# Memory attention's way out: a written-down DVE order, router logits first, the last tile's norm on ACT and POOL

## The chip, the cores and the metric

One core of a Trainium2 chip runs the whole program in one launch. The metric is device time in microseconds. The program is a two-layer encoder over 512 tokens of width 1024, in fp32.

## The reference, cut to what matters

```python
for i in range(DEPTH):                      # 2 layers
    mix = differential_attention(h, ...) if i % 2 == 0 else dsa_sparse_mla(h, ...)
    h = layer_norm(alpha * h + mix, ln_g[i, 0], ln_b[i, 0])
    h = layer_norm(alpha * h + memory_cross_attention(h, mem_k, mem_v, xa_w_q[i], xa_w_out[i]),
                   ln_g[i, 1], ln_b[i, 1])
    h = layer_norm(alpha * h + hierarchical_moe(h, ...), ln_g[i, 2], ln_b[i, 2])

def memory_cross_attention(x, mem_k, mem_v, w_q, w_out):
    ...                                     # o: softmax over 256 memory rows, 4 heads
    return o @ w_out                        # 512x1024 by 1024x1024

def hierarchical_moe(x, ...):               # 16 experts, two of them for each token
    g_logits = t @ w_group + b_group        # 4 columns
    e_logits = t @ w_expert + b_expert      # 16 columns
    ...
```

The place of the change is the second of the three norms: `o @ w_out`, the sum with `alpha * h`, the norm, and the 20 router logits of the normed row.

## The kernel before, in words

The 512 tokens are four tiles `t` of 128 rows, `hx[t]` (128x1024, fp32, named `xp0x` in layer 0 and `xp1x` in layer 1). A product in full precision is three TensorE products: each weight is split into a high half (ACT copies it to fp32r, L209) and a low half (DVE subtracts, L210); so are the activations. `U.get(name)` splits the next weight unit of a written list and issues the loads of the units behind it on SP's queue; a unit is 1 MB. Raw units share three buffers, those of the expert cells (`cell_r`) have these and two more, and a load waits until the split before it in its buffer is done. The units behind the output weights `w00`, `w01`, `w10`, `w11` are those of the first expert, `mw_0_0` and so on.

Queues of SP and POOL run in the order in which the code is written; DMAs issued there wait in that order too. The order of PE, ACT and DVE around the change is set by a planner that simulates the program, except inside blocks with `manual_schedule(engines=...)`: there the named engines run in written order. `mem_attention` has such a block for PE. At its end PE has already multiplied the first six of eight row blocks of `w_out`'s left half for all four tiles (`begun`).

`out_proj` then finishes the stage. For each half row `hf` and tile `t`: the rest of the product on PE (`proj_part`, L254 to L256, one 128x512 product each); on DVE the sum with `ALPHA * hx` and its row sums (L343, called a close below); `router_part`, which transposes the half row on PE (L673), copies it to SBUF (L678 on ACT for the left half, L676 on DVE for the right) and multiplies it with the router's weights on PE (L681). For the left half DVE keeps the 20 partial logits (L685). After the right half of a tile: `ln_stats` (mean on DVE, L301; Square with row sums on ACT, L305; `rsqrt` in nine small DVE steps, L193 to L202), `router_logits` (three small DVE steps, L689 to L691), `ln_scale` (DVE, 128x1024, L309), `ln_shift` (DVE for 768 columns, L315; POOL for the other 256 in two steps, L318 and L319), `after1` (a store to `h_d` on POOL's queue, L1556, and to `acc_d` on SP's, L1557), and for tiles 0 and 1 `pre`, which splits one unit of the first expert.

PSUM: `mm` tiles (two buffers) take the products of tiles 0 and 1 and all of the right half; tiles 2 and 3 of the left half share one `sc2` pair; `tp` tiles (two buffers) take transposes and logits.

`moe` follows. `router` (L720 to L751) is some 25 small DVE steps over all four tiles; `slot_tokens` makes the first two experts' token lists (L866 to L869), POOL fills the gather tiles (L911) and gathers their rows from `h_d` (L915), so the gather needs the last tile's store. PE turns the rows (L922) and the first expert starts (L937).

## Time and profile before

| | us |
|---|---|
| median of 3 runs (1708.81 to 1712.48) | 1708.97 |
| profiled execution | 1712.64 |
| its span | 1710.9 |
| PE busy | 1560.7 (91%) |
| DVE busy | 1179.8 (69%) |
| ACT busy | 845.5 (49%) |
| POOL busy | 233.7 (14%) |

Times in rows and text are microseconds from the start of the profiled span. PE is TensorE's products, DVE VectorE, ACT ScalarE, POOL GpSimd, SP the queue of SyncE. An engine's idle time counts only where the next stage waits for that engine.

### The profile page before, as it was taken

What the parts mean: (1) busy time and instruction counts of PE and PEld (TensorE: products, weight loads), DVE (VectorE), ACT (ScalarE), POOL (GpSimd) and SP (SyncE); (2) the same over time, 40 slices, a digit from 0 to 9 for tenths busy, and PEclk for the clock granted to TensorE, in tenths of its full rate; (3) what the DMA queues carried; (4) which work ended last, traced back from release to release, by engine and by line L of the source; (5) the groups of instructions that cost most, each with busy time, mean ns of one, the idle gap of its engine ahead of it and who ended that gap; (6) DMA issues with size and microseconds to landing.
All of it is one profiled execution on the core that took longest, in us unless ns stands there. A gap on an engine that the chain in (4) does not pass through costs nothing. (4 is left out here: it accounts for less than half of the span.)

```text
span 1710.9 us, 23216 instructions
## 1 busy us (share of the span) xinstructions
PE 1560.7 (91%) x8572; PEld 1298.0 (76%) x8572; DVE 1179.8 (69%) x2324; ACT 845.5 (49%) x1135; POOL 233.7 (14%) x230
## 2 busy tenths in 40 slices
PE   7999899798995899999997879998999599999995
PEld 6888698697774678888876747798878487888883
DVE  5444545645447898898867699737335899899695
ACT  4343544523331676785754434633332377577582
POOL 1000000111003032221210000002001223132121
PEclk9999899899997899999998989999999699999997
DMA  7130123622325698998975201115141699899894
GB/s 224 50 99 1 48 89 117 215 77 99 127 95 204 236 344 326 306 355 321 314 228 178 95 25 39 49 62 175 50 147 62 241 348 374 296 322 360 287 302 135
DMA packets 118334, 317.58 MB, mean 186 GB/s; under 512 B 23773, under 2 KB 72925, under 8 KB 93632
## 3 DMA queue, kind: packets, MB, share of 16 engines
q1 hardware_dynamic: 100400, 272.00, 45.0%
q0 software_dynamic: 17808, 43.96, 8.3%
q8 instruction: 71, 1.16, 0.3%
q14 instruction: 55, 0.45, 0.1%
HBM read 299.38 MB, written 36.70 MB: 196 GB/s over the span
## 5 line engine op out<-in xcount | busy, mean ns | idle before, releaser
L210 DVE TENSOR_TENSOR cell_l<-cell_r,cell_h 128x2048 fp32r<-128x2048 f32 x192 | 430.8, 2285 | 40.9 <-ACT cell_h L209 40.8
L209 ACT ACTIVATE cell_h<-cell_r 128x2048 fp32r<-128x2048 f32 x192 | 363.5, 1915 | 81.6 <-DMA cell_r<-in_moe_w_up_dram 19.8
L937 PE MATMUL pg<-cell_h,xh 128*128 128x512 f32 x288 | 119.2, 414 | 2.2 <-ACT xh L259 2.2
L965 PE MATMUL py<-cell_h,hsh 128*128 128x512 f32 x288 | 116.1, 403 | 1.4 <-ACTq L1065 1.4
L937 PE MATMUL pg<-cell_l,xh 128*128 128x512 f32 x288 | 116.0, 403 | 0.0
L965 PE MATMUL py<-cell_h,hsl 128*128 128x512 f32 x288 | 113.4, 394 | 0.0
L965 PE MATMUL py<-cell_l,hsh 128*128 128x512 f32 x288 | 113.1, 393 | 0.0
L937 PE MATMUL pu<-cell_h,xh 128*128 128x512 f32 x288 | 112.0, 389 | 0.0
L937 PE MATMUL pu<-cell_l,xh 128*128 128x512 f32 x288 | 112.0, 389 | 0.0
L955 POOL DMA_INDIRECT acc_d<-y,sx x34 | 74.8, 2200 | 156.9 <-ACT y L954 115.1
L915 POOL DMA_INDIRECT xg<-h_d,sx x32 | 42.0, 1312 | 358.1 <-DVE sx L902 328.4
L259 ACT ACTIVATE xh<-xgT 128x1024 fp32r<-128x1024 f32 x36 | 36.8, 1022 | 98.5 <-PE xgT L922 93.3
L937 PE MATMUL pg<-cell_h,xl 128*128 128x512 f32 x288 | 79.1, 397 | 0.0
L937 PE MATMUL pu<-cell_h,xl 128*128 128x512 f32 x288 | 77.0, 389 | 0.0
L937 PEld LDWEIGHTS pg<-cell_h,xh 128*128 128x128 f32 x288 | 56.6, 197 | 14.1 <-ACT xh L259 3.0
L937 PEld LDWEIGHTS pg<-cell_h,xl 128*128 128x128 f32 x288 | 55.7, 193 | 12.4
L937 PEld LDWEIGHTS pg<-cell_l,xh 128*128 128x128 f32 x288 | 56.5, 196 | 11.2
L965 PEld LDWEIGHTS py<-cell_h,hsh 128*128 128x128 f32 x288 | 54.5, 189 | 13.1 <-ACTq L1065 1.8
L965 PEld LDWEIGHTS py<-cell_h,hsl 128*128 128x128 f32 x288 | 54.5, 189 | 12.6 <-DVEq L1065 0.9
L965 PEld LDWEIGHTS py<-cell_l,hsh 128*128 128x128 f32 x288 | 54.6, 190 | 10.6
L937 PEld LDWEIGHTS pu<-cell_h,xh 128*128 128x128 f32 x288 | 54.1, 188 | 11.2
L937 PEld LDWEIGHTS pu<-cell_h,xl 128*128 128x128 f32 x288 | 54.1, 188 | 11.2
(917 smaller groups left out, 4206.1 us busy)
## 6 DMA issues: line engine op xcount, KB each, us to landing
cell_r<-in_moe_w_gate_dram SPq DMA_DIRECT2D x64, 1024.0 KB, 8.0
cell_r<-in_moe_w_up_dram SPq DMA_DIRECT2D x64, 1024.0 KB, 8.1
cell_r<-in_moe_w_down_dram SPq DMA_DIRECT2D x64, 1024.0 KB, 7.2
mhx<-acc_d POOLq DMA_DIRECT2D x8, 512.0 KB, 7.0
x<-in_x_dram SPq DMA_DIRECT2D x4, 512.0 KB, 6.9
g<-in_ln_g_dram POOLq DMA_DIRECT2D x4, 512.0 KB, 4.0
b<-in_ln_b_dram POOLq DMA_DIRECT2D x4, 512.0 KB, 4.0
op0x<-in_x_dram POOLq DMA_DIRECT2D x4, 512.0 KB, 7.6
```

Source lines behind the costliest of these rows:

```text
L209: nc.scalar.activation(hi[:, c], raw[:, c], AF.Copy)
L210: nc.vector.tensor_tensor(lo[:, c], raw[:, c], hi[:, c].bitcast(F32), op=ALU.subtract)
L259: nc.scalar.activation(hi, src, AF.Copy)
L915: nc.gpsimd.indirect_dma_start(out=x, out_offset=None, in_=h_d[:, :], in_offset=bass.IndirectOffsetOnAxis(ap=idx[:, 0:1], axis=0), bounds_ ...
L937: nc.tensor.matmul(o, xT[l][:, a, :], W[r][:, k, :], start=a == l == r == 0, stop=a == 7 and l == 1)
L955: nc.gpsimd.indirect_dma_start(out=acc_d[:, :], out_offset=bass.IndirectOffsetOnAxis(ap=ix[:, 0:1], axis=0), in_=y, in_offset=None, bounds ...
L965: nc.tensor.matmul(o, hs[a][:, ts(2 * q + f)], Dq[b][:, f, c], start=q == f == k == 0, stop=q == f == 1 and k == 2)
```

## The change

`xp_proj` takes the place of `out_proj` for memory attention's way out; `out_proj` stays for the other attentions and loses its options. In `xp_proj` DVE runs in written order: the four left halves with the kept logits and the splits of `w10`, `w11` and the first expert unit between them; then for each tile the right half, the mean, the scale and shift of the tile before (or, at tile 0, the split of the second expert unit), rsqrt and the router's logits. `router_part` copies both halves on ACT and returns its logits tile, which stays in PSUM until `keep` or `router_logits` reads it. The last tile is normed by ACT (`x * rstd + nmr`, where `nmr` is the negative mean times `rstd`) and POOL (times the gain, plus the bias, both 128x1024). The splits of the first expert units, and with them the loads that they issue, are written ahead of the stores.

```diff
--- before.py
+++ after.py
@@ -39,7 +39,6 @@
 DBL = (5, 11)
 HP = 400
 FILL = [["q2"], ["v1", "q3"], ["q4"], ["v2", "q5"], ["m0", "q6"], ["v3", "q7"], ["m1", "m2"], ["m3"]]
-NFIRST = 2
 RING = 6
 RAWS = 5
 DSA0 = ("P0", "P1", "F0 P2", "F1 P3")
@@ -295,15 +294,16 @@
         q.dma_start(b, I["ln_b"][i, j].partition_broadcast(P))
         return g, b
 
-    def ln_stats(hx, sums, name, eps=EPS):
+    def ln_mean(hx, sums, name):
         nmu = small(name + "m", [P, 1])
-        if len(sums) == 2:
-            nc.vector.tensor_scalar(nmu, sums[0], sums[1], -1.0 / D, op0=ALU.add, op1=ALU.mult)
-        else:
-            nc.vector.tensor_scalar(nmu, sums[0], -1.0 / D, None, op0=ALU.mult)
+        nc.vector.tensor_scalar(nmu, sums[0], sums[1], -1.0 / D, op0=ALU.add, op1=ALU.mult)
         ss = small(name + "s", [P, 1])
         nc.scalar.activation(junk, hx, AF.Square, bias=nmu, accum_out=ss)
-        return nmu, rsqrt(ss, 1, name, 1.0 / D, eps)
+        return nmu, ss
+
+    def ln_stats(hx, sums, name):
+        nmu, ss = ln_mean(hx, sums, name)
+        return nmu, rsqrt(ss, 1, name, 1.0 / D, EPS)
 
     def ln_scale(hx, nmu, gb):
         nc.vector.scalar_tensor_tensor(hx, hx, nmu, gb[0], op0=ALU.add, op1=ALU.mult)
@@ -323,36 +323,82 @@
         mm3(o, [(oT[0](k, ts(t)), oT[1](k, ts(t)),
                  W[k // 4][0][:, k % 4, :], W[k // 4][1][:, k % 4, :]) for k in ks], ks[0] == 0, last)
 
-    def out_proj(oT, src, ij, name, after, R=None, pre=None, begun=None):
+    def xp_proj(oT, src, i, after, R, split_first, begun):
+
+        name = f"xp{i}"
+        sums = [[small(f"{name}s{t}{hf}", [P, 1], bufs=2 * NT) for hf in range(2)] for t in range(NT)]
+        gb = load_gb(i, 1)
+        hx = reload(src, f"{name}x")
+        W, o, n0 = begun
+        half = [slice(0, 512), slice(512, D)]
+        lps, stats = {}, {}
+
+        def close(hf, t):
+            proj_part(o[t], oT, W, t, range(n0 if hf == 0 else 0, 8), True)
+            x = hx[t][:, half[hf]]
+            nc.vector.scalar_tensor_tensor(x, x, ALPHA, o[t], op0=ALU.mult, op1=ALU.add, accum_out=sums[t][hf])
+            lps[hf, t] = router_part(R, t, hf, x, f"{name}{t}{hf}")
+
+        def keep(t):
+            nc.vector.tensor_copy(R["lg"][:, t, :], lps.pop((0, t))[:, 0:20])
+
+        def apply(t):
+            ln_scale(hx[t], stats[t][0], gb)
+            ln_shift(hx[t], stats[t][1], gb)
+            after(t, hx[t])
+
+        with tc.manual_schedule(engines={ENG.DVE}):
+            close(0, 0)
+            close(0, 1)
+            W2 = [U.get(f"{name}w10")]
+            keep(0)
+            close(0, 2)
+            keep(1)
+            W2.append(U.get(f"{name}w11"))
+            close(0, 3)
+            keep(2)
+            split_first()
+            keep(3)
+            W, o = W2, {}
+            for t in range(NT):
+                o[t] = mm(f"{name}o1{t}")
+                close(1, t)
+                nmu, ss = ln_mean(hx[t], sums[t], f"{name}ln{t}")
+                if t:
+                    apply(t - 1)
+                else:
+                    split_first()
+                stats[t] = nmu, rsqrt(ss, 1, f"{name}ln{t}", 1.0 / D, EPS)
+                router_logits(R, t, stats[t], lps.pop((1, t)))
+
+            nmu, rstd = stats[t]
+            nmr = small(f"{name}nr", [P, 1])
+            nc.vector.tensor_tensor(nmr, nmu, rstd, op=ALU.mult)
+            nc.scalar.activation(hx[t], hx[t], AF.Identity, bias=nmr, scale=rstd)
+            nc.gpsimd.tensor_tensor(hx[t], hx[t], gb[0], op=ALU.mult)
+            nc.gpsimd.tensor_tensor(hx[t], hx[t], gb[1], op=ALU.add)
+            after(t, hx[t])
+
+    def out_proj(oT, src, ij, name, after):
         sums = [[small(f"{name}s{t}{hf}", [P, 1], bufs=2 * NT) for hf in range(2)] for t in range(NT)]
         gb = load_gb(*ij)
         hx = reload(src, f"{name}x")
         for hf in range(2):
-            early = begun if begun and hf == 0 else None
-            W = early[0] if early else [U.get(f"{name}w{hf}{q}") for q in range(2)]
+            W = [U.get(f"{name}w{hf}{q}") for q in range(2)]
             for t in range(NT):
-                o = early[1][t] if early else mm(f"{name}o{hf}{t}")
-                if begun:
-                    proj_part(o, oT, W, t, range(early[2] if early else 0, 8), True)
-                else:
-                    for q in range(2):
-                        mm3(o[:, q * 256:(q + 1) * 256],
-                            [(oT[0](k, ts(t)), oT[1](k, ts(t)),
-                              W[q][0][:, k, :], W[q][1][:, k, :]) for k in range(8)])
+                o = mm(f"{name}o{hf}{t}")
+                for q in range(2):
+                    mm3(o[:, q * 256:(q + 1) * 256],
+                        [(oT[0](k, ts(t)), oT[1](k, ts(t)),
+                          W[q][0][:, k, :], W[q][1][:, k, :]) for k in range(8)])
                 c = slice(hf * 512, hf * 512 + 512)
                 nc.vector.scalar_tensor_tensor(hx[t][:, c], hx[t][:, c], ALPHA, o, op0=ALU.mult, op1=ALU.add,
                                                accum_out=sums[t][hf])
-                if R:
-                    router_part(R, t, hf, hx[t][:, c], f"{name}{t}{hf}")
                 if hf == 1:
                     stats = ln_stats(hx[t], sums[t], f"{name}ln{t}")
-                    if R:
-                        router_logits(R, t, stats)
                     ln_scale(hx[t], stats[0], gb)
                     ln_shift(hx[t], stats[1], gb)
                     after(t, hx[t])
-                    if pre:
-                        pre(t)
 
     def reload(src, name, tags="abcd", q=nc.gpsimd, t0=0):
         hx = []
@@ -665,29 +711,23 @@
             nc.tensor.matmul(pc[:, 0:40], ones, wg[:, k, :], start=k == 0, stop=k == 7)
         nc.vector.tensor_copy(rc[:, 0:20], pc[:, 0:20])
         nc.vector.tensor_tensor(rc[:, 20:40], pc[:, 20:40], br, op=ALU.add)
-        return dict(w=wg, c=rc, lg=small(f"lgs{i}", [P, NT, 20]), lp=None)
+        return dict(w=wg, c=rc, lg=small(f"lgs{i}", [P, NT, 20]))
 
     def router_part(R, t, hf, x, nm):
         pt = tp(f"hTf{nm}")
         for j in range(4):
             nc.tensor.transpose(pt[:, ts(j)], x[:, ts(j)], ident)
         xT = t2("e", f"hTs{nm}")
-        if hf:
-            nc.vector.tensor_copy(xT, pt)
-        else:
-            nc.scalar.activation(xT, pt, AF.Copy)
+        nc.scalar.activation(xT, pt, AF.Copy)
         lp = tp(f"lg{nm}")
         for j in range(4):
             nc.tensor.matmul(lp[:, 0:20], xT[:, ts(j)], R["w"][:, 4 * hf + j, 0:20], start=j == 0, stop=j == 3)
-        if hf:
-            R["lp"] = lp
-        else:
-            nc.vector.tensor_copy(R["lg"][:, t, :], lp[:, 0:20])
-
-    def router_logits(R, t, stats):
+        return lp
+
+    def router_logits(R, t, stats, lp):
         lg, rc = R["lg"][:, t, :], R["c"]
         nc.vector.scalar_tensor_tensor(lg, rc[:, 0:20], stats[0], lg, op0=ALU.mult, op1=ALU.add)
-        nc.vector.tensor_tensor(lg, lg, R["lp"][:, 0:20], op=ALU.add)
+        nc.vector.tensor_tensor(lg, lg, lp[:, 0:20], op=ALU.add)
         nc.vector.scalar_tensor_tensor(lg, lg, stats[1], rc[:, 20:40], op0=ALU.mult, op1=ALU.add)
 
     def router(i, R):
@@ -1558,11 +1598,11 @@
 
         first = []
 
-        def pre(t):
-            if t < NFIRST:
-                first.append(U.get(f"mw{i}_{ORDER[t][0]}_{ORDER[t][1]}"))
-
-        out_proj(oT, h_d, (i, 1), f"xp{i}", after1, R, pre, begun)
+        def split_first():
+            p, j = ORDER[len(first)]
+            first.append(U.get(f"mw{i}_{p}_{j}"))
+
+        xp_proj(oT, h_d, i, after1, R, split_first, begun)
         gT, W3, D3 = [], [], []
 
         def before():
```

## Rows read from the trace of the kernel before

**Rows 1.** The page, its first part: busy time, share of the span and instructions of each engine.

```profile
PE 1560.7 (91%) x8572; PEld 1298.0 (76%) x8572; DVE 1179.8 (69%) x2324; ACT 845.5 (49%) x1135; POOL 233.7 (14%) x230
```

**Rows 2.** Stretches of the span: from, to (us); length; busy us (and instructions) of PE, of PE's weight loads, of DVE, of ACT and of POOL; granted clock of PE; share of the DMA engines; GB/s. First a piece of memory attention in layer 0, then three stretches of its way out and of the gather in layer 0, then two of layer 1.

```profile
440.00:470.00 30.00, 30.00 (x135) 23.71 (x134) 11.66 (x13) 8.89 (x16) 0.80 (x2) 1.00 0.36 126
...
494.85:528.20 33.35, 33.35 (x177) 28.38 (x177) 16.00 (x49) 6.89 (x10) 1.20 (x1) 1.00 0.10 33
...
528.20:542.20 14.00, 8.15 (x43) 7.00 (x42) 13.69 (x40) 2.37 (x4) 8.00 (x10) 0.61 0.85 320
...
542.20:552.14 9.94, 1.90 (x22) 1.29 (x22) 7.95 (x41) 0.00 (x0) 3.98 (x5) 0.50 0.96 394
...
1318.70:1332.40 13.70, 7.49 (x43) 6.49 (x42) 13.63 (x41) 2.39 (x4) 8.47 (x10) 0.66 0.84 315
...
1332.40:1342.46 10.06, 1.89 (x22) 1.28 (x22) 8.08 (x42) 0.00 (x0) 3.98 (x5) 0.50 0.98 406
```

**Rows 3.** DVE's timeline, layer 0, tail of the stretch: start (us), duration (us), engine, line, operation, out<-in, shapes, count, and in brackets the idle time before it and what ended it. The timelines below have the same columns.

```profile
528.16 0.69 DVE L343 SCALAR_TENSOR_TENSOR xp0x<-xp0x,xp0o 128x512 f32<-128x512 f32 x1 [0.15 <-PE xp0o L256]
...
541.12 0.24 DVE L691 SCALAR_TENSOR_TENSOR lgs<-lgs,rsyxp0ln,rc 128x20 f32<-128x20 f32 x1
...
542.21 0.16 DVE L720 TENSOR_REDUCE rt<-lgs 128x4 f32<-128x16 f32 x1
...
549.92 0.16 DVE L869 TENSOR_SCALAR ix<-pi 128x1 int32<-128x1 f32 x1 [0.28 <-PE pi L867]
```

**Rows 4.** POOL's timeline: the last store and the gather in layer 0, the gather in layer 1.

```profile
544.10 0.61 POOL L1556 DMA_DIRECT2D h_d<-xp0x  x1 [0.30 <-POOL xp0x L319]
...
552.14 1.08 POOL L915 DMA_INDIRECT xg<-h_d,ix  x1 [5.58 <-DVE rt L763]
...
1342.46 1.08 POOL L915 DMA_INDIRECT xg<-h_d,ix  x1 [5.70 <-DVE rt L764]
```

**Rows 5.** DMA. GB/s in 40 slices of the window from 520 to 562 us (1.05 us each); median us from issue to landing of the stores of `xp0x` in that window, and of the stores of `op0x` in the window from 381 to 412; two issues of weight loads on SP's queue.

```profile
GB/s 16 0 0 0 0 8 0 0 0 70 374 211 343 359 300 417 414 449 406 425 425 402 437 429 433 417 406 414 417 410 31 0 78 156 191 113 4 0 0 0
...
h_d<-xp0x POOLq DMA_DIRECT2D x4, 512.0 KB, 9.4
...
h_d<-op0x POOLq DMA_DIRECT2D x4, 512.0 KB, 3.3
...
530.40 1.24 SPq L234 DMA_DIRECT2D cell_r<-in_moe_w_gate_dram  x2
```

**Rows 6.** What single steps take, layer 0: DVE's timeline (the low half of a split, a close, a scale, a shift, the first and the last step of one rsqrt with the copy of logits between them), then one Square on ACT.

```profile
466.61 2.29 DVE L210 TENSOR_TENSOR xp0w10l<-xp0w10r,xp0w10h 128x2048 fp32r<-128x2048 f32 x1 [1.02 <-ACT xp0w10h L209]
...
497.88 0.69 DVE L343 SCALAR_TENSOR_TENSOR xp0x<-xp0x,xp0o 128x512 f32<-128x512 f32 x1 [0.67 <-PE xp0o L256]
...
516.93 0.15 DVE L193 TENSOR_SCALAR rsvxp0ln<-xp0ln1s 128x1 f32<-128x1 f32 x1 [1.08 <-ACT junk L305]
...
518.15 0.18 DVE L685 COPY lgs<-lgxp 128x20 f32<-128x20 f32 x1 [0.24 <-PE lgxp L681]
...
518.94 0.16 DVE L202 SCALAR_TENSOR_TENSOR rsyxp0ln<-rswxp0ln,rsyxp0ln 128x1 f32<-128x1 f32 x1
...
525.55 1.28 DVE L309 SCALAR_TENSOR_TENSOR xp0x<-xp0x,xp0ln0m,g 128x1024 f32<-128x1024 f32 x1
...
526.86 1.02 DVE L315 SCALAR_TENSOR_TENSOR xp0x<-xp0x,rsyxp0ln,b 128x768 f32<-128x768 f32 x1
...
533.40 1.15 ACT L305 ACTIVATE junk<-xp0x,xp0ln3m 128x1024 bf16<-128x1024 f32 x1 [4.07 <-issue]
```

**Rows 7.** PE's timeline, layer 0: transposes of a tile's first half row (L673), the first products of the second half row (L254 to L256), 19 more products left out, the logits of the first tile (L681), the next transposes.

```profile
499.05 0.60 PE L673 MATMUL hTfxp<-ident,xp0x 128*128 128x128 f32 x4
...
499.41 0.47 PE L254 MATMUL xp0o<-xp0w10h,xoTh 128*128 128x512 f32 x1
...
499.72 0.39 PE L255 MATMUL xp0o<-xp0w10l,xoTh 128*128 128x512 f32 x1
...
499.95 0.40 PE L256 MATMUL xp0o<-xp0w10h,xoTl 128*128 128x512 f32 x1
...
504.52 0.96 PE L681 MATMUL lgxp<-wg,hTsxp 128*128 128x20 f32 x8
...
505.33 0.63 PE L673 MATMUL hTfxp<-ident,xp0x 128*128 128x128 f32 x4
```

**Rows 8.** POOL's steps of `ln_shift` (L318, L319) and DVE's steps beside them, layer 0; one DVE step with POOL idle (515.61); one POOL fill of a whole tile.

```profile
515.61 0.24 DVE L689 SCALAR_TENSOR_TENSOR lgs<-rc,xp0ln1m,lgs 128x20 f32<-128x20 f32 x1
...
528.75 0.72 POOL L319 TENSOR_TENSOR xp0x<-xp0x,b 128x256 f32<-128x256 f32 x1
...
528.77 0.74 DVE L689 SCALAR_TENSOR_TENSOR lgs<-rc,xp0ln2m,lgs 128x20 f32<-128x20 f32 x1
...
541.27 1.73 POOL L318 TENSOR_SCALAR xp0x<-xp0x,rsyxp0ln 128x256 f32<-128x256 f32 x1 [0.68 <-DVE rsyxp0ln L202]
...
542.40 0.17 DVE L722 TENSOR_TENSOR rt<-lgs,rt 128x16 f32<-128x16 f32 x1
...
543.08 0.72 POOL L319 TENSOR_TENSOR xp0x<-xp0x,b 128x256 f32<-128x256 f32 x1
...
543.11 0.72 DVE L715 TENSOR_TENSOR rt<-iota,rt 128x16 f32<-128x16 f32 x1
...
554.56 0.96 POOL L911 MEMSET xg<- 128x1024 f32 x1
```

## The prediction

> **What bounds the kernel now.** First the page: PE is busy 91% of the span and DVE 69% [rows 1], so a gain must come from a stretch where PE is not fed. Second the stretch table: the way out of memory attention keeps PE full for 33 us at full clock, then DVE is full for 14 us while PE works at half clock, then PE has 1.9 us of work in 9.9 us [rows 2]; layer 1 shows the same two numbers within 0.3 us. From the last projection product to the gather of the first expert's tokens PE is nearly idle, so that stretch is priced one to one, in both layers.
>
> Third, DVE's timeline there. The last half-row sum (L343) starts at 528.16. `ln_scale` and `ln_shift` of three tiles and three copies of transposed rows are still queued, so the last router logits (L691) come at 541.12, the first router step (L720) at 542.21 and the first token list (L869) at 549.92 to 550.08 [rows 3]. Fourth, POOL's queue: the last `h_d` store issues at 544.10, the gather only at 552.14, 2.06 us after its token list was there [rows 4]. The gather reads `h_d`; the DMA rates show why it waits: some 400 GB/s from 530 until 551.5, then almost nothing [rows 5]. In that burst lie four loads of 1 MB and eight stores of 0.5 MB, 8 MB; at 400 GB/s that is 20 us, and an `h_d` store in it takes 9.4. So before, the last store's landing ends the stretch, with the router's chain 2 us behind it. Both must get shorter.
>
> **The change, part by part,** on layer 0's clock.
>
> *Loads.* The three loads that follow the first weight split, and the one behind the second, are now written ahead of all four `acc_d` stores on SP's queue; before they stood between them [rows 5]. They issue when raw buffers come free, from about 506 to 519 by the order below, and 4 MB at 400 GB/s is 10 us: done by about 525. The last `h_d` store then shares the queues with one `acc_d` store. The same store without load beside it lands in 3.3 us [rows 5]; I take that, and keep the 8.0 us of before (544.10 to 552.1) for a rival. The three `h_d` issues ahead of it stay where they are on POOL's queue.
>
> *First half.* `close(0,0)` and `close(0,1)` run as before, the second from 497.88 to 498.65. The low half of `w10`, which ran at 466.61 in an idle DVE [rows 6], now comes behind it: 2.29 us, to 500.9. PE has its first `w10` product at 499.4 and wants the low half at 499.7 [rows 7]: it waits, and fills part of it with a logits product (0.81 us). I price the rest at 0.8 us. DVE's own chain from there is short: four copies `keep` of 0.2 (L685), two closes of 0.77, `w11` and one expert split of 2.25 each, 6.8 us to 507.7. But each `keep` waits for transposes, an ACT copy and a logits product on PE, whose order a planner sets. Before, it put 22 products between a tile's transposes (499.05) and its logits (504.52), though ACT's copy takes 0.60 [rows 7]: it takes products for cheaper than they are. Now only 54 products exist before `close(1,0)` (six of tile 3, 48 of the two open tiles). I take 46 of them ahead of the fourth logits product: 46 x 0.23 = 10.6, three transposes of 0.36 and three more logits of 0.81: 14.1 us [rows 7]. `close(1,0)` starts at about 515.2. Bounds: 508 (order prompt, DVE's chain) and 519 (all 54 ahead, and PE idle 2 us for `w11`, which is queued behind `keep(1)`).
>
> *Second half.* In written order DVE does for a tile: close 0.73 and mean 0.3, the second split 2.2 (tile 0) or the previous tile's scale and shift 1.31 + 0.94, rsqrt 2.17 with a 0.3 us copy wedged in, so 1.9, and three logit steps 0.55: 5.7 us [rows 6]. ACT's Square (1.15) hides behind scale and shift, the copy of transposed rows is now on ACT, 0.60, idle there. From tile 1 on POOL's `+ b` holds up some small DVE step, 0.5 to 0.7 us (below); I take 0.6. `close(1,3)` starts at 515.2 + 5.7 + 2 x 6.3 = 533.5. PE alone would be there at 532.5: it ended at 528.1, plus 0.8, plus three logits and two transposes that before came later (3.2), plus 0.35 of wait. So DVE sets it. Each logits result keeps one of the two small PSUM buffers until DVE has taken it, and PE's next logits product, with all products queued behind it, waits for that; here DVE is there first, and rival (b) prices it if not. Behind it 6.3 and `nmr` 0.15: 540.0. The router starts there, 2.2 us earlier than before, not 14.
>
> *The last tile's norm.* Its scale and shift (2.25) leave DVE. ACT's pass, bounded by Square on the same size, takes 1.15 [rows 6] and POOL starts at 541.5. The trace has no POOL product of 128x1024. The nearest row is 128x256 in 0.72 us [rows 8]: four times is 2.9; a fill of 128x1024, which reads nothing, takes 0.96. I take 2.6 each, nearer to the same operation. The store issues 0.3 behind, at 547.0, and lands at 550.3.
>
> What do these passes do to DVE? When POOL's 128x256 sum began at 543.08, DVE's L715 began at 543.11 and took 0.72 instead of 0.2; L689 took 0.74 under the sum at 528.75, and 0.24 alone [rows 8]. A DVE step with two SBUF inputs waits until such a sum is over. Under POOL's one-input product (541.27 to 543.00) L722 took its 0.17 [rows 8]: that form doesn't hold it. The new passes have two inputs and are four times as wide, and nearly all router steps have two. So: from 540.0 the router runs 1.8 us, waits to the first pass's end at 544.15, does one step, waits to 546.95. It loses 4.9 us. Undisturbed it needs 7.87 us from L720 to the token list, of which 0.55 was L715's wait: 7.3. The list is there at 540.0 + 7.3 + 4.9 = 552.2, the gather at 552.35. The store (550.3) is hidden behind it. POOL's fills of the gather tiles stand ahead of the gather as before and end by 549.5.
>
> [...]
>
> **The sum.** Before, the gather was at 552.14, now 552.35: +0.2. Layer 1 is the same code; its stretch is 0.2 us shorter up to the gather [rows 2, 4], so +0.3. The splits that leave memory attention (two low halves of 2.29) give nothing there, since DVE ran them while PE was full [rows 2, 6]; without that cover they would give 4.6. Edits that only pass names around cost nothing. The profiled execution took 1712.64, its span 1710.9; the median of the runs is 1708.97. The shift is small against either: 1708.97 + 0.5 = **1709.5 us**. What the runs can tell from no change I take as 0.2%, 3.4 us.
>
> **Rivals.** (a) *POOL's passes hold DVE little*, say because small steps slip in between, as L722 did under L318. Then the store's landing ends the stretch: 540.0 + 7.0 + 3.3 + 0.1 = 550.4, 1.7 us a layer: 1705.6. With PE's order prompt too (`close(1,3)` at 532.5, 1.0 earlier) it is 1703.6. Speaks against: L715 and L689. Prompt order alone gives 1707.5.
> (b) *Logits late on PE.* DVE's order is now fixed, so one late logits product delays `close(1,t)` and all behind it. If `close(1,0)` starts at 519 and the second half waits 1 us more, the router starts at 545 and the gather is at 557: +4.9 a layer, 1719. From 516.7 on it shows as slower. The 22 products of [rows 7] speak for it, the few products that are left against.
> (c) *The store lands last.* Were the store to take 8.0 us as in the burst, the gather is at 555.1: 1715. It decides from 5.2 us on. The loads' place speaks against it.
> (d) *POOL's one-input steps (L318) stop DVE's steps too,* 0.92 us for each of tiles 0 to 2, the 1.73 at 541.27 being 0.8 of wait and 0.9 of work: 2.8 a layer, 1715. L722's row speaks against it. [...]
>
> **Chances.** Forecast with prompt order beside it (within 0.2%): 0.42. Faster, mostly (a): 0.31. Slower: (b) 0.17, (c) 0.06, (d) 0.04, together 0.27. The forecast's own range is 1706 to 1712.5; the range that takes in (a) with prompt order and most of (b) is 1703.5 to 1717.5.
>
> **What the new profile should show.** No expert loads after 525 and a DMA rate that falls between stores. `close(1,0)` near 515 and `close(1,3)` near 533.5, DVE idle under 3 us between them. The first router step near 540 and two router steps of about 2.4 us each, just inside POOL's two passes of 2.3 to 2.9 us. The gather waiting on DVE's token list, not on `h_d`. Wrong if router steps run through POOL's passes (a), if DVE idles on `lgxp` between closes (b), or if the gather waits over 1 us behind the list (c).

## The result and the profile after

The change made the kernel slower: 1723.47 us (median of 5 runs, 1721.37 to 1726.23) against 1712.48 for the kernel before on the same chip, ratio 1.0075 [1.0062, 1.0087]. The forecast was no change, 1709.5. The profiled execution after took 1722.15 us, its span 1720.4.

Executions differ by a few us ahead of the stage, so both traces are read from the stage's own start, the first close (496.52 before, 493.01 after). In us behind it, layer 0:

| | 5th close | 8th close | router's first step | gather | gather, layer 1 |
|---|---|---|---|---|---|
| before | 11.33 | 31.64 | 45.69 | 55.62 | 55.42 |
| forecast | 18.7 | 37.0 | 43.5 | 55.8 | about as layer 0 |
| after | 21.15 | 43.49 | 49.68 | 62.00 | 63.55 |

The gathers come 6.4 and 8.1 us late, 14.5 in all. That is the loss: 0.75% of 1712 is 12.8, and the two medians are 11.0 apart.

The page's first part has hardly moved from [rows 1]; the loss is seen only in its stage.

```profile
PE 1555.2 (90%) x8572; PEld 1293.0 (75%) x8572; DVE 1179.1 (69%) x2315; ACT 852.3 (50%) x1144; POOL 240.3 (14%) x230
```

Stretches of the changed kernel, with the columns of [rows 2]: the stage in layer 0 piece by piece, then a piece of layer 1.

```profile
493.00:514.00 21.00, 20.71 (x114) 17.15 (x113) 9.74 (x14) 4.31 (x5) 0.00 (x0) 1.00 0.45 162
515.00:523.00 8.00, 6.91 (x36) 5.83 (x36) 4.98 (x16) 1.73 (x3) 0.00 (x0) 1.00 0.85 306
523.00:531.00 8.00, 6.90 (x36) 5.86 (x36) 5.45 (x16) 1.73 (x3) 3.02 (x3) 1.00 0.33 132
531.00:543.00 12.00, 5.51 (x24) 4.70 (x24) 10.84 (x38) 3.63 (x7) 6.00 (x6) 0.54 0.29 118
...
1320.40:1323.80 3.40, 3.40 (x10) 2.64 (x9) 3.08 (x12) 0.78 (x3) 2.68 (x3) 0.51 0.00 0
```

Before, PE was full for 33 us and then DVE for 14 [rows 2]. Now PE is full only for the first half. After it neither engine is: from 515 to 531 PE stands 2.19 us and DVE 5.57 of 16, each in turn, and from 531 the last two tiles go through DVE with PE at half clock (0.54). DVE's timeline shows the turns.

```profile
514.07 0.18 DVE L343 COPY lgs<-lgxp 128x20 f32<-128x20 f32 x1 [4.32 <-PE lgxp L724]
514.16 0.68 DVE L339 SCALAR_TENSOR_TENSOR xp0x<-xp0x,xp0o 128x512 f32<-128x512 f32 x1
521.95 0.17 DVE L730 TENSOR_TENSOR lgs<-lgs,lgxp 128x20 f32<-128x20 f32 x1 [2.71 <-PE lgxp L724]
522.31 0.68 DVE L339 SCALAR_TENSOR_TENSOR xp0x<-xp0x,xp0o 128x512 f32<-128x512 f32 x1
530.08 0.17 DVE L730 TENSOR_TENSOR lgs<-lgs,lgxp 128x20 f32<-128x20 f32 x1 [2.16 <-PE lgxp L724]
530.44 0.68 DVE L339 SCALAR_TENSOR_TENSOR xp0x<-xp0x,xp0o 128x512 f32<-128x512 f32 x1
536.50 0.68 DVE L339 SCALAR_TENSOR_TENSOR xp0x<-xp0x,xp0o 128x512 f32<-128x512 f32 x1
542.69 0.17 DVE L760 TENSOR_REDUCE rt<-lgs 128x4 f32<-128x16 f32 x1
544.53 2.03 DVE L749 TENSOR_TENSOR rt<-rt,rt 128x64 f32<-128x64 f32 x1
546.59 2.38 DVE L750 SCALAR_TENSOR_TENSOR rt<-rt,iota 128x64 f32<-128x64 f32 x1
553.99 0.16 DVE L909 TENSOR_SCALAR ix<-pi 128x1 int32<-128x1 f32 x1 [0.28 <-PE pi L907]
```

And PE's timeline, the transposes (L719) and logits (L724) of the second half; the products between them are left out.

```profile
515.00 0.63 PE L719 MATMUL hTfxp<-ident,xp0x 128*128 128x128 f32 x4 [0.96 <-DVE xp0x L339]
...
520.95 0.96 PE L724 MATMUL lgxp<-wg,hTsxp 128*128 128x20 f32 x8
523.15 0.63 PE L719 MATMUL hTfxp<-ident,xp0x 128*128 128x128 f32 x4 [1.24 <-DVE xp0x L339]
...
529.08 0.96 PE L724 MATMUL lgxp<-wg,hTsxp 128*128 128x20 f32 x8
```

This is a ring. PE runs a tile's transposes, 24 products of a later tile and only then the tile's logits (520.95). DVE must take those logits (L730) before it may do the next close (L339), by the written order. PE's next step is that close's transposes, so it stands 1.24 us. The close itself had nothing left to wait for: the 54 products that were open before the fifth close, all 48 of the right half's first two tiles among them, are recorded before 513. One turn is 8.13 us (522.31 to 530.44), where before a close came every 6.77.

POOL's timeline answers to [rows 4], the rates of DMA (520 to 562 us) to [rows 5].

```profile
544.14 2.33 POOL L378 TENSOR_TENSOR xp0x<-xp0x,g 128x1024 f32<-128x1024 f32 x1 [1.95 <-ACT xp0x L377]
546.56 2.34 POOL L379 TENSOR_TENSOR xp0x<-xp0x,b 128x1024 f32<-128x1024 f32 x1
549.19 0.59 POOL L1596 DMA_DIRECT2D h_d<-xp0x  x1 [0.30 <-POOL xp0x L379]
...
555.01 1.09 POOL L955 DMA_INDIRECT xg<-h_d,ix  x1 [3.38 <-DVE oh L906]
```
```profile
GB/s 390 258 55 8 0 0 0 176 347 402 82 0 0 0 0 289 347 363 0 0 0 386 339 273 0 0 0 0 285 351 363 0 0 0 0 78 191 219 55 0
...
h_d<-xp0x POOLq DMA_DIRECT2D x4, 512.0 KB, 4.2
```

The loads are out of the way: the rate falls to nothing between stores, and a store lands in 4.2 us (median) instead of 9.4. So that part of the change did what it says.

### The profile page after: what moved, and what is told of

Its sections match the earlier page's. It is cut to its first block, busy times and chain, and to the rows that moved or that the text cites. A ratio compares the mean times of both kernels' runs of the same rounds, so it can differ in the third digit from the quotient of the medians.

```text
span 1720.4 us, 23234 instructions
## 1 busy us (share of the span) xinstructions
PE 1555.2 (90%) x8572; PEld 1293.0 (75%) x8572; DVE 1179.1 (69%) x2315; ACT 852.3 (50%) x1144; POOL 240.3 (14%) x230
## 5 line engine op out<-in xcount | busy, mean ns | idle before, releaser
L977 PEld LDWEIGHTS pu<-cell_l,xh 128*128 128x128 f32 x288 | 54.1, 188 | 11.2
```

What stands on the lines that cost most here:

```text
L977: nc.tensor.matmul(o, xT[l][:, a, :], W[r][:, k, :], start=a == l == r == 0, stop=a == 7 and l == 1)
```

## The experiments

Theory T: DVE's written order ties DVE to logits that the planner lets PE run late. Rival S: the four splits in that order cost the time. Rival L: the last tile's norm on ACT and Pool costs it, by the DVE steps that Pool holds up (two of them, 2.03 and 2.38 us in the changed kernel) and by the later store. All ratios are to the kernel before, from runs on the same chip; where the intervals of two runs overlap, their times alone don't tell the two apart. The table at the end shows the stage of each run.

**One step moved.** In the changed kernel, tile t's logits go behind the sum of tile t+1:

```diff
-        def close(hf, t):
+        def close(hf, t, late=None):
...
+            if late is not None:
+                router_logits(R, late, stats[late], lps.pop((1, late)))
...
-                close(1, t)
+                close(1, t, t - 1 if t else None)
...
-                router_logits(R, t, stats[t], lps.pop((1, t)))
+            router_logits(R, t, stats[t], lps.pop((1, t)))
```

> The changed kernel, but the router's logits of tile t stand in DVE's order behind the sum of tile t+1 (behind `close(1,t+1)`) instead of in front of it; nothing else is moved. Theory T (DVE's written order waits for logits products that PE runs behind the next tile's 24 products): DVE can take the sum of tile t+1 as soon as its products are there, frees its bank, and PE need not stand idle in front of the next transposes. In the changed kernel the logits took DVE's waits of 2.71, 2.16 us (layer 0) and 2.69, 3.78 us (layer 1); I expect about 3.7 us less from the stage's first close to the router's first step in layer 0 and about 5 us less in layer 1, and a time near 1714 to 1716 us where the changed kernel has 1723. Rival S (the four splits written into DVE's order are what costs): nothing changes, 1722 to 1724 us. [...]

Measured 1719.71 us, 1.0052 [1.0034, 1.0069]. The router starts 48.58 us behind the first close in both layers, 1.1 and 2.7 earlier than in the changed kernel: right in sign, a third and a half of the size that T named. PE no longer stands ahead of the transposes of tile 1, but DVE's wait has not gone, it has moved: the sum of tile 1 is done at 520.41, and then DVE stands 3.69 us for the logits of tile 0 (524.25), with the whole normalization of tile 0 queued behind them. (Part of the 3.69 is PE's clock, 0.63 from 515 to 518.5 in this run.)

```profile
519.72 0.68 DVE L339 SCALAR_TENSOR_TENSOR xp0x<-xp0x,xp0o 128x512 f32<-128x512 f32 x1
...
524.25 0.17 DVE L732 TENSOR_TENSOR lgs<-lgs,lgxp 128x20 f32<-128x20 f32 x1 [3.69 <-PE lgxp L726]
```

S wanted no change before the router, and what L blames all lies behind its first step; the traces show a change ahead of that, but the interval of the ratio overlaps that of the changed kernel, so the time alone decides nothing. Moving this one DVE step did not end the waits, with PE still running the logits behind 24 products.

**The norm back on DVE**, in the changed kernel:

```diff
-            nmu, rstd = stats[t]
...
-            nc.scalar.activation(hx[t], hx[t], AF.Identity, bias=nmr, scale=rstd)
-            nc.gpsimd.tensor_tensor(hx[t], hx[t], gb[0], op=ALU.mult)
-            nc.gpsimd.tensor_tensor(hx[t], hx[t], gb[1], op=ALU.add)
-            after(t, hx[t])
+            apply(t)
```

> The changed kernel, but the last tile's normalization is done on DVE as for the other three tiles (two steps of 1024 columns in front of the router) instead of ACT and Pool. Rival L (the norm on ACT and Pool costs it): the two Pool passes held two small steps of the router for 2.03 and 2.38 us, and the h_d store came to be the last thing that the gather waited for (0.86 us behind the token list). Without them the router starts 2.3 us later (two DVE steps of some 1.15 us) but loses no 4.4 us, and the store is some 3 us earlier: the gather comes about 2 us sooner in each layer, 1718 to 1720 us in all. If L were the whole cause of the loss it would come back to the time of before, 1711 to 1713. Theory T (waits for the logits on PE): no more than those 2 us per layer, because the waits of the two halves all stand ahead of the norm.

Measured 1724.66 us, 1.0079 [1.0060, 1.0098]: nothing came back, where 1718 to 1720 was expected, so L is not the cause of the loss. From the router's first step to the gather it takes 9.66 us instead of 12.32, as expected, but the router's start swings: 53.95 us behind the first close in layer 0, 50.75 in layer 1. In layer 0 PE's granted clock was 0.83 from 519 to 539 us, and that eats the gain; in layer 1, at 1.00 from 1318 to 1335, the gather is 3.2 us sooner than in the changed kernel.

**PE's order written as well,** in both halves; shown is the second.

```diff
-        with tc.manual_schedule(engines={ENG.DVE}):
...
+        with tc.manual_schedule(engines={ENG.DVE, ENG.PE}):
...
+                prod(1, t)
+                sum_(1, t)
+                if t + 1 < NT:
+                    prod(1, t + 1, 8)
+                turn(1, t)
...
+                if t + 1 < NT:
+                    prod(1, t + 1, 8)
+                logit(1, t)
```

> The changed kernel, but PE's order of the stage is written down as well as DVE's: the transposes and logits products of a tile are put between products of the next tile (8 products, transposes, 8 products, logits, 8 products) instead of where the planner puts them, behind all 24. Theory T: DVE's waits in front of the logits of the second half go (2.71 and 2.16 us in layer 0, 2.69 and 3.78 us in layer 1), a part of the 9.8 us of waits in the first half goes too, and PE no longer stands idle in front of the transposes; the router starts some 8 us sooner in each layer than in the changed kernel, the gather comes some 2 us sooner than in the kernel before: about 1706 to 1710 us. Rival S (splits in DVE's order): DVE is as late as before its splits, 1720 to 1724. Rival L (norm on ACT and Pool): 1720 to 1724 as well, since that part is not touched.

Measured 1704.79 us, 0.9979 [0.9962, 0.9996]. Same DVE order with its four splits, same norm, only PE's order differs, and the loss is gone. The router starts at 41.71 in both layers, 8.0 and 9.6 us sooner than in the changed kernel (some 8 was expected), and layer 0's gather comes at 54.02. The time is a little below the 1706 to 1710 that T named.

```profile
493.00:508.00 15.00, 15.00 (x92) 13.13 (x91) 9.82 (x15) 4.31 (x5) 0.00 (x0) 1.00 0.52 176
508.00:515.00 7.00, 7.00 (x38) 5.90 (x37) 5.18 (x16) 1.84 (x3) 0.00 (x0) 1.00 1.01 427
515.00:522.00 7.00, 7.00 (x38) 5.89 (x38) 5.66 (x17) 1.83 (x3) 3.00 (x3) 1.00 0.40 165
```

In these stretches of that run PE has no gap, and DVE's 5.2 to 5.7 us of work a tile lie under it.

**The early splits alone**, in the kernel before:

```diff
         for hf in range(2):
...
+            if pre and hf == 1:
+                for t in range(NFIRST):
+                    pre(t)
...
-                    if pre:
-                        pre(t)
```

> The kernel before with a single part of the change: the two splits of the next stage's first weights are written at the start of the second half instead of behind its first two tiles. The planner keeps the order of DVE. Theory T says that the change's own idea costs nothing by itself and that the loss is the written order: DVE's splits move out of the second half, which was DVE-bound, so the router's first step and the gather come up to 2 us sooner in each layer, bounded by the token list: 1708 to 1712 us against 1712 for the kernel before. Rival S (taking the splits early is what costs, because they hold up the first half's closes or their loads collide with others): slower than the kernel before by several us, towards 1718 or more.

Measured 1705.81 us, 0.9982 [0.9969, 0.9994]. The gain is there but not where it was expected: the router starts at 45.36 instead of 45.69, so DVE's 4.6 us of splits were never in its way. The time is below the 1708 to 1712 that was expected. The gather is at 54.08: 0.3 us of the gain are the router's, and 1.2 are that the gather now follows its token list by 0.86 us instead of 2.06. DMA had nothing left to move when the list was there:

```profile
540.00:544.00 4.00, 0.41 (x10) 0.34 (x10) 3.09 (x14) 0.00 (x0) 2.47 (x3) 0.50 0.66 262
544.00:547.00 3.00, 1.49 (x13) 0.94 (x12) 2.27 (x13) 0.00 (x0) 0.15 (x1) 0.50 0.00 0
```

The gather was issued at 546.85, and DMA had been idle since 544; before, its share was 0.96 up to the gather [rows 2]. S falls: two of the splits are early here without a loss, and in the run before all four stood in the written order without one.

**PE's order and the norm on DVE together:**

> Both of the last experiments' edits at once: PE's order written down, and the last tile normalized on DVE. With PE's order written the router's first step came 41.7 us behind the stage's first close and the gather 54.0 us behind it (55.6 in the kernel before). With the norm on DVE the gather followed the router's first step by 9.6 us instead of 12.3. If the two costs lie one behind the other on the same chain (theory T with the shared port as a second cost), they add: router's first step at some 42.9 us, gather at some 52.5 us, 3.1 us per layer sooner than in the kernel before, so about 0.3 to 0.4% faster than it (1703 to 1706 us where it has 1710). If the norm on ACT and Pool is worth what it takes (rival), this is no faster than the run with PE's order alone: ratio 0.998.

Measured 1702.06 us, 0.9950 [0.9934, 0.9967]; router 42.79, gather 52.46, as expected; the time is a little below the 1703 to 1706 named. The two costs add.

**The written order taken away**, all else as in the changed kernel:

```diff
-        with tc.manual_schedule(engines={ENG.DVE}):
+        if True:
```

> The changed kernel with every part of it but one: DVE's order is not written down, the planner places the steps. Theory T, as the first experiments leave it (the stage is PE-bound; a DVE order that waits for a logits product lets PE stand, and then PE's clock falls): PE is busy without gaps again from the first close to the eighth, as in the kernel before (31.6 us there, 43.5 us in the changed kernel). The norm on ACT and Pool still costs the router 4 us. Router's first step 43 to 46 us behind the first close, gather 54 to 57 us: a ratio of 0.997 to 1.003 to the kernel before. Rival L (the norm on ACT and Pool is what costs): the ratio stays near 1.0075.

Measured 1706.36 us, 0.9977 [0.9965, 0.9989]; 8th close 31.61, router 42.04, gather 54.01. One line of the change makes 1.0075 out of 0.9977, 1% of the time. L falls a second time.

**The norm alone**, in the kernel before, for the last tile:

```diff
-                    ln_scale(hx[t], stats[0], gb)
-                    ln_shift(hx[t], stats[1], gb)
+                    if R and t == NT - 1:
...
+                        nc.scalar.activation(hx[t], hx[t], AF.Identity, bias=nmr, scale=stats[1])
+                        nc.gpsimd.tensor_tensor(hx[t], hx[t], gb[0], op=ALU.mult)
+                        nc.gpsimd.tensor_tensor(hx[t], hx[t], gb[1], op=ALU.add)
```

> The kernel before with one part of the change alone: the last tile is normalized on ACT and Pool. The router starts up to 2.8 us sooner, since DVE loses two steps of 1.75 and 1.01 us, and loses 4.0 us in its two held steps, so the token list comes some 1.2 us later. The h_d store is issued some 3 to 4 us later (two Pool passes of 2.33 us); in the kernel before it took 8.0 us to land, because the DMA queues were full of the next stage's weights, and the gather waited for it. If the store's wait stays 8 us (theory: this part costs), the gather comes 3 to 4 us later in each layer, about 1717 us. If the weights' loads are the bound and drain at the same time in any case (rival), the gather comes some 1 us later, 1712 us and a ratio within 1.002.

Measured 1714.40 us, 1.0026 [1.0014, 1.0037]. The gather comes 1.0 and 1.2 us later, the rival's number, but the runs lost 4.2 us by the medians, between the two; both forecasts missed. In layer 0 the router starts 2.1 us sooner and its chain to the list is 3.35 us longer.

**The copies on ACT**, with the early splits, in the kernel before:

```diff
-        if hf:
-            nc.vector.tensor_copy(xT, pt)
-        else:
-            nc.scalar.activation(xT, pt, AF.Copy)
+        nc.scalar.activation(xT, pt, AF.Copy)
```

> The kernel before with two parts of the change: the two splits of the next stage's first weights ahead of the second half, as in the run with early loads (ratio 0.998), and the copies of the second half's transposes on ACT instead of DVE. With early loads alone DVE was busy without a gap from the eighth close to the router's first step (13.7 us), and PE's logits products waited 1.1, 1.7 and 1.1 us for those copies. Theory T's reading (here, behind the last products, DVE is the bound): without its copies of 0.68 us DVE is 2.0 to 2.7 us sooner at the router, and the gather, which waited for the token list, follows: another 2 us per layer, 1702 to 1704 us where the kernel before has 1710, ratio about 0.996. Rival (ACT's copy stands behind its Square of 1.15 us and the logits come as late as before): no change against the run with early loads, 0.998.

Measured 1703.68 us, 0.9961 [0.9947, 0.9974]; router 43.99, gather 52.81. Against the early splits alone the router is 1.4 us sooner in layer 0 and 1.8 in layer 1, where T said 2.0 to 2.7: right in kind, DVE is the bound behind the last product, but smaller.

**Which half of the written order.** First the second half alone, by the edit shown, then the first half alone, by its complement:

```diff
-        with tc.manual_schedule(engines={ENG.DVE}):
+        if True:
             close(0, 0)
...
             W, o = W2, {}
+
+        with tc.manual_schedule(engines={ENG.DVE}):
             for t in range(NT):
```

> The changed kernel, with DVE's order written down for the second half (and the norm) alone; the planner places the first half's closes, keeps and splits. With no order written at all the fifth close came 11.3 us behind the first, the eighth 31.6 and the ratio to the kernel before was 0.998; with all of it written 21.2, 43.5 and 1.0075. Theory F (the first half's keeps, which wait for logits that PE runs behind the next half's products, cost most): the fifth close comes back to about 11.3 us; PE may still stand in the second half in front of the transposes, about 2 us per tile (8.1 us apart against 6.8), so the eighth close at some 35 us, the gather at some 56 us, ratio 1.000 to 1.003. Theory G (the logits in front of the next close in the second half cost most, the first half's waits being covered by PE's products): little comes back, ratio 1.006 or more.

> The complement: DVE's order is written down for the first half alone, the planner places the second half and the norm. Theory F: the fifth close stays at about 21 us behind the first; PE has done the products of the second half's first tile in that time, so a part of the 10 us comes back, as long as PE has products that it can run without a bank that DVE has yet to empty; the eighth close at some 21.2 + 3 x 6.8 = 41.5 us, gather at some 60 us or more, ratio 1.005 to 1.007. Theory G: the fifth close's lateness is made good by the planner's second half, the gather comes at some 54 to 56 us, ratio 0.998 to 1.001.

Measured 1724.35 us, 1.0078 [1.0065, 1.0091], with the second half written; 1708.04 us, 0.9983 [0.9967, 1.0000], with the first. Theory F falls, G holds. DVE's timeline of the first of the two runs:

```profile
510.31 0.69 DVE L339 SCALAR_TENSOR_TENSOR xp0x<-xp0x,xp0o 128x512 f32<-128x512 f32 x1
...
520.61 0.18 DVE L343 COPY lgs<-lgxp 128x20 f32<-128x20 f32 x1 [4.76 <-PE lgxp L726]
...
524.66 0.18 DVE L343 COPY lgs<-lgxp 128x20 f32<-128x20 f32 x1 [3.87 <-PE lgxp L726]
...
526.96 0.18 DVE L732 TENSOR_TENSOR lgs<-lgs,lgxp 128x20 f32<-128x20 f32 x1 [2.12 <-PE lgxp L726]
527.32 0.68 DVE L339 SCALAR_TENSOR_TENSOR xp0x<-xp0x,xp0o 128x512 f32<-128x512 f32 x1
```

The fifth close comes at 11.30, as early as before, and it helps nothing: the sixth stands 17 us behind it, because the logits of tile 0 (526.96) must be taken first. The two kept logits ahead of them (L343), which the planner placed there, make nothing worse: PE runs tile 0's logits behind both. In the other run:

```profile
512.02 0.68 DVE L339 SCALAR_TENSOR_TENSOR xp0x<-xp0x,xp0o 128x512 f32<-128x512 f32 x1
...
513.10 0.69 DVE L339 SCALAR_TENSOR_TENSOR xp0x<-xp0x,xp0o 128x512 f32<-128x512 f32 x1
...
526.66 0.69 DVE L339 SCALAR_TENSOR_TENSOR xp0x<-xp0x,xp0o 128x512 f32<-128x512 f32 x1
```
```profile
512.00:527.00 15.00, 15.00 (x85) 12.84 (x83) 12.92 (x48) 5.45 (x9) 5.73 (x6) 1.00 0.78 324
```

The fifth close comes 7.5 us late (18.86) and it costs nothing. The sixth follows 1.08 us behind: the planner lets DVE do both closes in a row and the logits later. Both engines are busy at once, PE without a gap and DVE for 12.92 of 15 us. In layer 1 of this run the last two tiles' logits ran at half clock (1.90 and 1.89 us instead of 0.96; the granted clock is 0.60 from 1312 to 1322), and the gather there came at 55.39 instead of 52.49.

**Two combinations** of edits shown above, the planner's order or the first half's order, each with the norm back on DVE:

> The changed kernel without its written order and without its norm on ACT and Pool: what stays is the early splits, the copies on ACT and the place of the logits' steps in the program. With the planner's order and the norm on ACT and Pool the router's first step came 42.0 us behind the first close, the gather 54.0 (ratio 0.998). Theory (the shared port is a cost of its own, 4.0 us on the router's two held steps): the router starts up to 2.3 us later and the gather follows it by 9.6 us instead of 12.0, so it comes at 53 to 54 us: 0.1 to 1 us per layer sooner, ratio 0.996 to 0.998. Rival (the norm on ACT and Pool is worth it when nothing else waits): the gather comes later than 54.0 us, ratio 0.998 or more.

> The changed kernel with DVE's order written down for the first half alone, as in the run before it, and the last tile normalized on DVE. With the norm on ACT and Pool that order gave the router's first step 40.5 us (layer 0) and 43.4 us (layer 1) behind the first close and the gather 52.5 and 55.4 us behind it. If the norm's price is the same here (the router up to 2 us later, the gather 9.6 us behind it instead of 12.0), the gather comes at 51 to 52 us in layer 0: 0.2 to 0.6% faster than the kernel before, ratio 0.994 to 0.997, and no better than the planner's order with the norm on DVE (0.995) by more than 0.1%. Rival (early splits written in front of the fifth close are worse than the planner's place for them): gather at 53 us or more, ratio 0.997 or more.

Measured 1701.62 us, 0.9952 [0.9938, 0.9965], and 1701.98 us, 0.9933 [0.9909, 0.9957]: some 0.5 to 0.7% faster than the kernel before. With PE's order and the norm on DVE (0.9950) these are the best versions, and their intervals don't tell the three apart. With the planner's order the gather is sooner than the 53 to 54 that was expected. Against the same orders with the norm on ACT and Pool the gather is 1.5 us (planner's order) and 1.4 us (first half written) sooner in layer 0.

The stage in all runs, in us behind the first close, layer 0 (the gather in both layers):

| run | 5th close | 8th close | router | gather | layer 1 | ratio |
|---|---|---|---|---|---|---|
| before | 11.33 | 31.64 | 45.69 | 55.62 | 55.42 | 1 |
| changed kernel | 21.15 | 43.49 | 49.68 | 62.00 | 63.55 | 1.0075 |
| logits one step later | 21.15 | 41.83 | 48.58 | 60.89 | 60.85 | 1.0052 |
| changed, norm on DVE | 21.15 | 46.70 | 53.95 | 63.61 | 60.37 | 1.0079 |
| PE's order written | 14.93 | 35.53 | 41.71 | 54.02 | 53.98 | 0.9979 |
| PE's order, norm on DVE | 14.92 | 35.52 | 42.79 | 52.46 | 52.42 | 0.9950 |
| before, splits early | 11.33 | 31.64 | 45.36 | 54.08 | 54.35 | 0.9982 |
| ... and copies on ACT | 11.30 | 31.61 | 43.99 | 52.81 | 52.69 | 0.9961 |
| before, norm alone | 11.31 | 31.62 | 43.60 | 56.65 | 56.65 | 1.0026 |
| planner's order | 11.30 | 31.61 | 42.04 | 54.01 | 54.08 | 0.9977 |
| second half written | 11.30 | 43.13 | 49.31 | 61.61 | 61.61 | 1.0078 |
| first half written | 18.86 | 33.50 | 40.46 | 52.49 | 55.39 | 0.9983 |
| planner's order, norm on DVE | 11.30 | 31.62 | 43.70 | 52.52 | 52.81 | 0.9952 |
| first half written, norm on DVE | 18.84 | 33.49 | 42.33 | 51.07 | 50.85 | 0.9933 |

The 8th close alone says little: in layer 0 it is 1.9 us later with the first half written than with the planner's order, and the router starts 1.6 us earlier.

## Why the prediction was wrong

**The step that failed is the second half.** The sum had 5.7 + 2 x 6.3 = 18.3 us from the fifth close to the eighth, "So DVE sets it", with the late logits left to rival (b). Measured: 8.15, 8.13 and 6.06, together 22.34. DVE's own work was priced about right (6.06 against 6.3 in the last turn, where it waits for nothing); what was missing are its two waits for logits, 2.71 and 2.16. The prediction took the later of two finishing times, 533.5 for DVE and 532.5 for PE, each summed as if that engine never waited for the other, where the order makes them take turns. It said that DVE is at the logits first, and DVE was. That DVE then stands, with the next close behind the logits in its order and PE's transposes behind that close, the sum put at nothing.

**The first half** was sized short too: 46 of 54 products ahead of the fourth logits, where the trace has all 54 (8 x 0.23 is 1.8 us). The fifth close came at 517.7 on the clock of before, 2.5 behind the 515.2 of the sum and inside its bound of 519. But the runs show that this lateness is not the loss. With the first half alone written, PE was busy for 18.77 of the first 19 us, and layer 0's gather came 3 us sooner than before. With the second half alone written the fifth close came 9.9 us sooner than in the changed kernel, and the gather only 0.4. The prediction carried this lateness one to one to the router. (The 0.60 of ACT's copy, which it reads from [rows 7], is not in that group; the trace of before has it at L678.)

**Rival (b) happened**, with 0.17 given to it: router at 546.2 on the clock of before (it said 545), 1719 us against 1723. The prediction's own sign of it came too: DVE stood 4.87 us for `lgxp` between those closes, not under 3. Of the 14.0 us between 1709.5 and 1723.47, 3.5 are the base: 1708.97 was the median of three runs of the kernel before, 1712.48 is that of five. (b)'s sizes were the other way round: 3.8 us from the first half and 1 from the second, measured 2.5 and 4.0, so its time came out near in part by luck. Its condition, logits late on PE, was read from [rows 7] and then set aside ("the few products that are left against"). The second half had 48 products left, and those were enough.

**The router and POOL's passes: right.** Two steps were held, 2.03 and 2.38 us (forecast 4.9 us lost in all; less some 0.22 that each takes unheld, as in the run with the norm on DVE, it is 4.0). That a shared port is what holds them, as two of the expectations have it, no run shows; shown are these times under POOL's passes. The passes took 2.33 and 2.34 us against 2.6; no row of before gives the 2.3 at the low end of the range named for them. Router to list's end took 11.46 us against 12.2. Rivals (a) and (d) did not happen.

**The store: right in kind.** It isn't the last to arrive. The gather is issued 0.86 us behind the end of its list's step; it is the same 0.86 with the early splits alone and with PE's order and the norm on DVE, though there the store was issued 6.8 and 6.6 us ahead of the gather and not 5.8. So 0.86 is taken, as an estimate, to be the handoff, where the sum had 0.15, and rival (c) did not happen. In the run with the norm alone, whose loads are late, it is 1.83 in layer 0, as it was 2.06 before [rows 3, 4].

**What the rest of the change is worth.** The forecast set the norm's cost against the gain of the other parts and came to no change. The runs show both. Splits early, copies on ACT and the logits' place give 0.5% when the planner orders DVE and the norm stays on DVE; the logits' place can't be told from nothing in it (0.9952 against 0.9961 without it). Against it stand the norm on ACT and Pool, 0.25 to 0.5% in the four pairs of runs that differ in it alone and have PE full, and the written second half, 1%.

**Open:** why the norm alone lost 4.2 us when its two gathers were 2.3 us late (the interval of its ratio reaches down to 2.4 us, so this may be noise); and how the planner chooses PE's order once DVE's is fixed, which was only seen from outside.

## What to carry to other kernels

When one engine's order is written by hand and another's is left to a planner, follow the ring between the two queues: for each wait in the written order, ask what the other engine has queued ahead of the thing waited for, and what it has queued behind the thing that is held up. Here both orders written, neither written, or only the half in which PE stayed fed all did without the loss. Putting a wait for a late result behind everything that feeds the other engine should help as well, but that is not shown: one step moved back by one close gave 1.1 and 2.7 us. A late step cost little here while one of the two engines stayed full: with the first half written the fifth close came 7.5 us late, PE was busy for 15.00 of the 15 us from 512 to 527, and layer 0's gather came 3.1 us sooner than before. Read it from the stretch table, two engines with gaps in one stretch being the sign (PE 2.19 and DVE 5.57 of 16 us in the changed kernel).

## What the runs showed of the hardware

Behind the same short stand PE's granted clock fell in one layer, to 0.51, and stayed at 1.00 in the other. In the changed kernel PE stood 1.24 us ahead of the transposes of tile 1 in both layers; layer 1's is this:

```profile
1319.27 0.63 PE L719 MATMUL hTfxp<-ident,xp1x 128*128 128x128 f32 x4 [1.24 <-DVE xp1x L339]
```

In layer 0 the stretch behind it, 523 to 531, ran at 1.00. In layer 1, 1320.4 to 1323.8 ran at 0.51, and the turn took 9.74 us instead of 8.13. In the run with the norm on DVE it was layer 0's turns that grew so, to 9.75 and 9.74 us, at 0.83 from 519 to 539. So behind the same stand a turn was 1.6 us longer in one layer and no longer in the other, and that is 1.6 of layer 1's 8.1 us. What decides it no run shows.

Under POOL's wide two-input passes some DVE steps stood and others did not. DVE's timeline in the run with the norm alone, under passes at 538.57 and 540.98 (2.33 and 2.41 us):

```profile
538.64 2.29 DVE L731 TENSOR_SCALAR rt<-rt 128x16 f32<-128x16 f32 x1
...
541.23 0.22 DVE L737 TENSOR_REDUCE rt<-rt 128x4 f32<-128x64 f32 x1
541.48 1.99 DVE L716 TENSOR_TENSOR rt<-rt,rt 128x64 f32<-128x64 f32 x1
```

A step with one input (L731) was held as long as one with two, which the prediction had not thought of: 2.29 us, where the same step took 0.17 before (L724), and 1.99 for the one with two (L716), 0.22 before (L709). A reduction (L737) ran through in 0.22 us, as before (L730). What sets them apart no run shows.
